# Second Hyena layer's intermediates in PSUM, and the seams of the one-stream layers

## The chip, the cores and the metric

One core of a Trainium2 chip runs the program once per execution. The metric is the device time of one execution in microseconds (us); the time before is the median of three runs. A profiled execution is a run by itself, with its own time.

## What is computed

A diffusion trunk of four layers over 256 latent tokens and 256 context tokens of width 1024, batch 1. Layers 0 and 3 mix tokens by a Hyena long convolution, layer 1 by gated linear attention, layer 2 by latent attention (MLA); an MLP follows each. Context tokens are last read in layer 2, so its MLP and all of layer 3 run on one stream, the 256 latent tokens. In short:

```python
for i in range(4):
    x = x + gate1[i] * mixer(modulate(rmsnorm(x), shift1[i], scale1[i]))
    x = x + gate2[i] * (relu(modulate(rmsnorm(x), shift2[i], scale2[i]) @ w1[i]) ** 2) @ w2[i]
out = rmsnorm(x) * final_g

def hyena(u):                      # layer 3: u is (256, 1024)
    z = short_conv(u @ w_in + b_in)            # three taps along the tokens, 3 x 1024 channels
    y, gates = z[:, :1024], (z[:, 1024:2048], z[:, 2048:])
    for n in range(2):
        y = gates[n] * (irfft(rfft(y, 512) * spectrum[n], 512)[:256] + y * skip[n])
    return y @ w_out + b_out
```

All inputs are fp32.

## The kernel before

**Layout.** x is kept transposed in SBUF, eight tiles `x0` to `x7` (`xT[k]`) of 128 channels x tokens. A product of fp32 accuracy is three matmuls: each operand is split into a rounded high part and the rest (`H` and `L`), and `mm3` (L368) adds high x high, high x rest and rest x high. `split` (L174) makes the parts: ScalarE casts, VectorE subtracts. Weights come as slabs of 128x1024 (`wload`): SP's DMA into `wraw`, a cast on ScalarE (L359, `wh`), a subtraction on GpSimd (L360, `wl`). PSUM's eight banks are dealt out by tags: two `mm`, three `cv`, one `ada`, two `st`. The compiler's scheduler sets each engine's order from the program's order and priorities; the order stands in the program, and every engine works through its own queue.

**One-stream norm.** `lone_norm` (before each of the three one-stream sub-layers) does not wait for 1/rms: it makes u = x * scale (parts `uH`, L553 on ScalarE, and `uL`, L554 on VectorE), squares x on ScalarE (L490), adds the squares on VectorE (`sacc`, L497), sums over channels by four small matmuls (L501), works out 1/rms on small tiles, and spreads it over the partitions by a matmul of `ones` with a diagonal matrix (L557), copied to `rs`. Each product of u and a weight has two columns more, for the shift; `modulated` then multiplies by `rs` (L567).

**Updates of x.** `residual` multiplies the mixer's output by the output weights, a bank `mm` for each 128 channels, and adds into x in SBUF (L600). In the one-stream MLP the second product is summed in four banks (`sum`, two halves of 256 each) over all 32 hidden slabs, and added into x in SBUF at the end (L677).

**Second Hyena layer.** `project` makes, for a unit of 256 channels, six products of 24 matmuls: VectorE scales into `zb` in SBUF (L567), ScalarE adds the bias (L880) and starts the convolution (L881), VectorE adds the two outer taps (L884, L886) into `z`. `order` transposes z (L912, L913 make `zf`), transforms it by matmuls with `dftf`, multiplies by the spectrum `S` on VectorE (L956, L957 into `pr`), subtracts and adds on GpSimd (L958, L959), splits into `VH`, `VL`, transforms back with `dftg` into a bank `st`, and gates (L983 to L985; L991 in the second order). Four units run in steps: step n projects unit n + 1, runs order 0 of unit n and order 1 of unit n - 1, and `residual` follows as units end.

## Time and profile before

| | |
|---|---|
| median of 3 runs | 2227.89 us (2223.2 to 2237.05) |
| the profiled execution | 2229.64 us, span 2227.9 us |
| TensorE (PE) busy | 2081.7 us, 93% |
| VectorE (DVE) busy | 1339.7 us, 60% |
| GpSimd (POOL) busy | 1122.9 us, 50% |
| ScalarE (ACT) busy | 907.9 us, 41% |
| from the end of MLA to the last MLP | 1640 to 2050 us of the span |

The shares are means over stages with different limits. The rows further down are of the trace of this one execution; times in them count from the start of its span. Matmuls are pipelined, and a matmul's row overlaps the next one's. A "wait" of an engine names the instruction that ended it.

### The profile page before, as it was taken

How to read it: one execution, taken by the hardware profiler on the slowest of the kernel's cores; microseconds unless marked ns; L12 is line 12 of the kernel's file. 1: busy time of each engine (PE TensorE's matmuls, PEld its weight loads, DVE VectorE, ACT ScalarE, POOL GpSimd, SP SyncE). 2: the span in 40 equal slices, each digit the busy share in tenths (PEclk: the TensorE clock that was granted, in tenths of full speed). 3: DMA queues.
4: the chain of work that ended last, by engine and by line, in shares of the span. 5: the costliest groups of instructions: out<-in, count | busy, mean ns of one | idle time of the engine just before them, and what ended most of it. 6: DMA issues, size and time to landing. Idle time of an engine off the chain costs nothing. (4 is left out here: it accounts for less than half of the span.)

```text
span 2227.9 us, 33311 instructions
## 1 busy us (share of the span) xinstructions
PE 2081.7 (93%) x12834; PEld 1773.8 (80%) x12834; DVE 1339.7 (60%) x2412; ACT 907.9 (41%) x1505; POOL 1122.9 (50%) x669
## 2 busy tenths in 40 slices
PE   6998999899999999998999999999989997887998
PEld 3765687677888888877778787788779997877998
DVE  7864887765333345555666976777662227995223
ACT  2642333343333335544442222236445445544544
POOL 5662454256544434322234434443347887674885
PEclk8998999999999999999999999999999997998999
DMA  9675735534333333222137797743236664343663
GB/s 300 198 222 189 228 99 180 193 94 123 97 109 108 96 77 96 60 66 66 48 103 228 216 306 242 252 142 91 73 104 180 181 189 138 117 121 90 189 186 114
DMA packets 322302, 329.12 MB, mean 148 GB/s; under 512 B 21277, under 2 KB 248674, under 8 KB 322144
## 3 DMA queue, kind: packets, MB, share of 16 engines
q1 hardware_dynamic: 321012, 326.05, 47.4%
q8 instruction: 101, 1.65, 0.3%
q10 hardware_dynamic: 587, 0.61, 0.1%
q14 instruction: 58, 0.47, 0.1%
q0 software_dynamic: 544, 0.34, 0.1%
HBM read 317.51 MB, written 9.44 MB: 147 GB/s over the span
## 5 line engine op out<-in xcount | busy, mean ns | idle before, releaser
L360 POOL TENSOR_TENSOR wl<-wraw,wh 128x1024 fp32r<-128x1024 f32 (+2 forms) x378 | 912.6, 2428 | 891.8 <-ACT wh L359 821.1
L359 ACT CAST wh<-wraw 128x1024 fp32r<-128x1024 f32 (+2 forms) x378 | 391.1, 1043 | 613.5 <-PE mm L370 245.7
L370 PE MATMUL mm<-uL,wh 128*128 128x512 f32 (+3 forms) x1288 | 454.3, 354 | 12.0 <-DVE uL L530 6.5
L369 PE MATMUL mm<-uH,wh 128*128 128x512 f32 (+3 forms) x1288 | 454.0, 356 | 11.4 <-DVE zb L567 5.1
L371 PE MATMUL mm<-uH,wl 128*128 128x512 f32 (+3 forms) x1288 | 450.5, 351 | 0.0
L369 PEld LDWEIGHTS mm<-uH,wh 128*128 128x128 f32 (+1 forms) x1288 | 249.4, 195 | 54.0 <-issue 12.8
L370 PEld LDWEIGHTS mm<-uL,wh 128*128 128x128 f32 (+1 forms) x1288 | 250.5, 195 | 46.4 <-DVE uL L530 10.7
L371 PEld LDWEIGHTS mm<-uH,wl 128*128 128x128 f32 (+1 forms) x1288 | 250.9, 195 | 32.3 <-issue 3.8
L369 PE MATMUL cv<-fH,wh 128*128 128x512 f32 (+1 forms) x576 | 210.0, 370 | 9.7 <-ACT fH L176 6.9
L370 PE MATMUL cv<-fL,wh 128*128 128x512 f32 (+1 forms) x576 | 210.7, 367 | 0.7 <-DVE fL L177 0.6
L371 PE MATMUL cv<-fH,wl 128*128 128x512 f32 (+1 forms) x576 | 208.9, 366 | 0.0
L600 DVE SCALAR_TENSOR_TENSOR x<-cv,mods,x 128x256 f32<-128x256 f32 x256 | 112.5, 479 | 83.9 <-PE cv L371 83.9
L370 PE MATMUL sum<-fL,wh 128*128 128x256 f32 x512 | 138.6, 278 | 0.0
L369 PE MATMUL sum<-fH,wh 128*128 128x256 f32 x512 | 137.1, 278 | 0.0
L371 PE MATMUL sum<-fH,wl 128*128 128x256 f32 x512 | 136.9, 278 | 0.0
L369 PEld LDWEIGHTS cv<-fH,wh 128*128 128x128 f32 x576 | 108.2, 189 | 32.0 <-ACT fH L176 8.5
L369 PE MATMUL mm<-oH,wh 128*128 128x256 f32 (+1 forms) x288 | 102.6, 358 | 23.7 <-DVE x L600 18.1
L648 DVE SCALAR_TENSOR_TENSOR mm<-mm,r 128x512 f32<-128x512 f32 x60 | 41.8, 696 | 136.7 <-ACT r L647 136.7
L370 PEld LDWEIGHTS cv<-fL,wh 128*128 128x128 f32 x576 | 108.6, 189 | 19.1 <-DVE fL L177 1.1
L371 PEld LDWEIGHTS cv<-fH,wl 128*128 128x128 f32 x576 | 108.6, 189 | 17.7 <-issue 0.2
L436 DVE SCALAR_TENSOR_TENSOR st<-lw,sT,st 128x512 f32<-128x512 f32 x144 | 101.7, 750 | 9.6 <-DMA lw<-in_ada_w_dram 9.6
L564 DVE COPY rbias<-st 128x1 f32<-128x1 f32 x32 | 5.1, 158 | 162.7 <-PE st L371 162.5
(479 smaller groups left out, 4561.9 us busy)
## 6 DMA issues: line engine op xcount, KB each, us to landing
wraw<-in_mlp_w_dram SPq DMA_DIRECT2D x256, 512.0 KB
adaw<-in_ada_w_dram SPq DMA_DIRECT2D x96, 512.0 KB
lw<-in_ada_w_dram SPq DMA_DIRECT2D x96, 512.0 KB
wraw<-in_hy_w_in_dram SPq DMA_DIRECT2D x48, 512.0 KB
wraw<-in_gla_w_in_dram SPq DMA_DIRECT2D x24, 512.0 KB
spec<-S SPq DMA_DIRECT2D x16, 512.0 KB
wraw<-in_hy_w_out_dram SPq DMA_DIRECT2D x16, 512.0 KB
S<-spec SPq DMA_DIRECT2D x32, 256.0 KB
```

The lines of the kernel that those rows point to most:

```text
L359: nc.scalar.copy(wh[r0:r1, :n], raw[r0:r1, :n])
L360: nc.gpsimd.tensor_tensor(wl[r0:r1, :n], raw[r0:r1, :n], rounded(wh[r0:r1, :n]), ALU.subtract)
L369: nc.tensor.matmul(ps, lh, rh, start=start, stop=False)
L370: nc.tensor.matmul(ps, lh, rl, start=False, stop=False)
L371: nc.tensor.matmul(ps, ll, rh, start=False, stop=stop)
L436: nc.vector.scalar_tensor_tensor(dst, wt[:, cols], sT[:, k, 0:1], run[b], ALU.mult, ALU.add)
L564: nc.vector.tensor_copy(bias, ps[:, SEQ : SEQ + 1])
L600: add = nc.vector.scalar_tensor_tensor(xT[dt][:, q], ps[:, q], mods[i][:, gi, dt, r : r + 1], xT[dt][:, q], ALU.mult, ALU.add)
L648: nc.vector.scalar_tensor_tensor(r, r, 0.0, pos, ALU.max, ALU.mult)
```

## The change

In layer 3's Hyena (`not two` in the code), `zb` is the product's own bank: the scaling, the bias and the taps read and write it there. The product with the spectrum writes its first half to an SBUF tile of half the size and its second half back into the bank of the transform; the subtraction and addition, on VectorE now, end in that bank, and it is split from there. The gated product and the last product likewise stay in their `st` banks. `off` is made in the two-stream layer alone.

At the end of MLA and of Hyena `residual_lone` sums the last 256 rows of the output product in the four `sum` banks. There, and at the end of layer 2's MLP, `add_gated` writes the new x into the bank in place of SBUF (`fresh`), and `lone_norm` reads it from there: `uH`, `uL`, the squares (summed in a bank `mm`), and a copy of each tile to SBUF on ScalarE. `statistics` and its `rstd` are functions now, and `behind_norm` calls them so that the statistics come behind the first product and the matmul of 1/rms behind the third. The steps on the products that need `rs` follow it. The last MLP still adds into SBUF.

```diff
+    def add_gated(i, gi, sums, dt, in_place):
+        for e in (dt - 1, dt):
+            sv = sums[dt // 2][:, e % 2]
+            nc.vector.scalar_tensor_tensor(sv if in_place else xT[e][:, :SEQ], sv, mods[i][:, gi, e, 0:1],
+                                           xT[e][:, :SEQ], ALU.mult, ALU.add)
+            if in_place:
+                fresh[e] = sv
+    def residual_lone(i, gi, wmat, r0, fH, fL):
+        sums = pairs()
...
+                for k in range(2):
+                    mm3(sums[dt // 2][:, dt % 2], wh[:, k, cols], wl[:, k, cols], fH[k][:, :SEQ], fL[k][:, :SEQ],
+                        k == 0 and dt % 2 == 0, k == 1 and dt % 2 == 1)
+                if dt % 2 == 1:
+                    add_gated(i, gi, sums, dt, True)
     def lone_norm(i, which, mp):
...
-            nc.scalar.activation(uH[k][:, :SEQ], xT[k][:, :SEQ], AF.Copy, scale=sc)
-            nc.vector.scalar_tensor_tensor(uL[k][:, :SEQ], xT[k][:, :SEQ], sc, rounded(uH[k][:, :SEQ]),
+            nc.scalar.activation(uH[k][:, :SEQ], fresh[k], AF.Copy, scale=sc)
+            nc.vector.scalar_tensor_tensor(uL[k][:, :SEQ], fresh[k], sc, rounded(uH[k][:, :SEQ]),
                                            ALU.mult, ALU.subtract)
-        rb = bank("st")
-        nc.tensor.matmul(rb[:, :SEQ], ones, token_diag(token_rstd(0)), start=True, stop=True)
+        run = bank("mm")[:, :SEQ]
+        acc = np_.tile([P, SEQ], F32, tag="sacc", name=nm("sacc"), bufs=1)
+        for k in range(KD):
+            sq = np_.tile([P, SEQ], F32, tag="sq", name=nm("sq")) if k else None
+            nc.scalar.activation(sq if k else run, fresh[k], AF.Square)
+            if 0 < k < KD - 1:
+                nc.vector.tensor_tensor(acc if k == KD - 2 else run, run, sq, ALU.add)
+        for k in range(KD):
+            nc.scalar.copy(xT[k][:, :SEQ], fresh.pop(k))
...
+    def behind_norm(products, statistics, rest):
+        made = [products[0]()]
+        rstd = statistics()
+        made += [p() for p in products[1:]]
+        rstd()
+        return [rest(m) for m in made]
...
+                def convolved(made):
...
+                    zb = (mp.tile([P, 512], F32, tag="zb", name=nm("zb")) if two else ps)[:, :nt]
...
                         else:
+                            pr = mq.tile([P, 2, 256], F32, tag="pr1", name=nm("pr"))
+                            re, im = (pv[:, e : e + 1].broadcast_to([P, 2, 2, P]) for e in range(2))
+                            nc.vector.tensor_tensor(pr.rearrange("p r (a c) -> p r a c", a=2), re, s1, ALU.mult)
+                            nc.vector.tensor_tensor(pv, im, s2, ALU.mult)
+                            V2 = ps.rearrange("p (r c) -> p r c", r=2)
+                            nc.vector.tensor_tensor(V2[:, 0], pr[:, 0], V2[:, 0], ALU.subtract)
+                            nc.vector.tensor_tensor(V2[:, 1], pr[:, 1], V2[:, 1], ALU.add)
+                            split(V2, VH, VL)
...
+                            nc.vector.tensor_tensor(pr, even, gate, ALU.mult)
+                            nc.vector.tensor_tensor(eo, odd, gate[:, 1::-1], ALU.mult)
+                            nc.vector.tensor_tensor(eo, pr, eo, ALU.add)
+                            split(eo, *mids[cts[0]])
                     else:
+                        y = z[2] if two else acc
...
-                        split(z[2], h, l)
+                        split(y, h, l)
...
+                                if n == units - 1:
+                                    residual_lone(i, 2, g["hy_w_out"][j], n * 2 * P, *f)
...
-                    residual(i, 2, g["mla_wo"][j], pair * 2 * VD, oH, oL, SEQ)
+                    residual_lone(i, 2, g["mla_wo"][j], pair * 2 * VD, oH, oL)
```

**The order on PE at seam 1** (end of MLA into layer 2's MLP). Before, PE has this around the matmul of 1/rms; `mm_14944` and `mm_15026` are the first two products of the MLP, `st_14985` the third:

```order
L371 MATMUL mm_14944<-uH_14853,wl_14939 128x258
L369 MATMUL mm_15026<-uH_14851,wh_15020 128x258
L370 MATMUL mm_15026<-uL_14859,wh_15020 128x258
L371 MATMUL mm_15026<-uH_14851,wl_15021 128x258
L369 MATMUL mm_15026<-uH_14852,wh_15020 128x258
L370 MATMUL mm_15026<-uL_14860,wh_15020 128x258
L371 MATMUL mm_15026<-uH_14852,wl_15021 128x258
L369 MATMUL mm_15026<-uH_14853,wh_15020 128x258
L370 MATMUL mm_15026<-uL_14861,wh_15020 128x258
L371 MATMUL mm_15026<-uH_14853,wl_15021 128x258
L557 MATMUL st_14894<-diag_14931,ones 128x256
L369 MATMUL st_14985<-uH_14846,wh_14979 128x258
```

In the changed kernel PE has the end of the first product (`mm_14928`), the four statistics matmuls, and the start of the second product (`st_14976`):

```order
L370 MATMUL mm_14928<-uL_14857,wh_14923 128x258
L371 MATMUL mm_14928<-uH_14849,wl_14924 128x258
L603 MATMUL st_14953<-ones,sacc_14891 128x2
L603 MATMUL st_14953<-ones,sq_14911 128x2
L603 MATMUL st_14953<-ones,sacc_14891 128x2
L603 MATMUL st_14953<-ones,sq_14911 128x2
L369 MATMUL st_14976<-uH_14842,wh_14971 128x258
```

and, 48 rows behind the statistics, the end of the third product (`mm_15007`), 1/rms and the start of the fourth:

```order
L369 MATMUL mm_15007<-uH_14849,wh_15002 128x258
L370 MATMUL mm_15007<-uL_14857,wh_15002 128x258
L371 MATMUL mm_15007<-uH_14849,wl_15003 128x258
L610 MATMUL st_14953<-diag_14967,ones 128x256
L369 MATMUL st_15070<-uH_14842,wh_15065 128x258
```

The statistics stood some 37 matmuls behind the first product's start, with 11 left to do before 1/rms; now they stand 24 behind it, with 48 in between. Seam 3 has the same pattern.

**The order on ScalarE at seam 2** (layer 2's MLP into Hyena). Before, the last dozen rows up to the last square, which reads the last x tile; `wh` are casts of weights:

```order
L553 ACTIVATE uH_17231<-x_185,adam_11771 128x256
L553 ACTIVATE uH_17232<-x_186,adam_11771 128x256
L490 ACTIVATE sq_17285<-x_183 128x256
L1032 ACTIVATE x_181<-x_181,gb_18275 128x256
L490 ACTIVATE sq_17288<-x_184 128x256
L1032 ACTIVATE x_182<-x_182,gb_18278 128x256
L176 CAST dftf_17319<-traw_17321 128x512
L176 CAST dftg_17325<-traw_17327 128x512
L490 ACTIVATE sq_17291<-x_185 128x256
L359 CAST wh_17495<-wraw_17494 128x1024
L359 CAST wh_17534<-wraw_17533 128x1024
L490 ACTIVATE sq_17294<-x_186 128x256
```

Now, in the same place (L584 makes `uH`, L592 squares, L596 copies x to SBUF, L1145 adds the output bias):

```order
L176 CAST dftg_17315<-traw_17317 128x512
L584 ACTIVATE uH_17236<-sum_15149,adam_11771 128x256
L592 ACTIVATE sq_17289<-sum_15148 128x256
L592 ACTIVATE sq_17292<-sum_15148 128x256
L596 COPY x_183<-sum_15148 128x256
L596 COPY x_184<-sum_15148 128x256
L1145 ACTIVATE x_181<-x_181,gb_18266 128x256
L1145 ACTIVATE x_182<-x_182,gb_18269 128x256
L176 CAST dftg_17315<-traw_17321 128x512
L592 ACTIVATE sq_17295<-sum_15149 128x256
L359 CAST wh_17499<-wraw_17498 128x1024
L592 ACTIVATE sq_17298<-sum_15149 128x256
```

The copies have come in between; one weight cast fewer stands ahead of the last square, and that square is one row behind a cast whose buffer the first product frees.

**The order on VectorE in Hyena**, at the third product of unit 2 (`mm_17975` before, `mm_17969` now). Before, the product's bank is read for the last time by L567; `zb_17976` is in SBUF:

```order
L566 TENSOR_TENSOR zbias_18001<-mm_17975,params 128x1
L567 TENSOR_TENSOR zb_17976<-mm_17975,rs_17314 128x256
L956 TENSOR_TENSOR pr_18221<-cv_18214,S_18129 128x512
L957 TENSOR_TENSOR pr_18221<-cv_18214,S_18129 128x512
L886 SCALAR_TENSOR_TENSOR z_17889<-zb_17936,params,z_17889 128x255
L177 TENSOR_TENSOR VL_18198<-pr_18192,VH_18197 128x512
L912 TENSOR_TENSOR zf_18459<-z_17889 128x256
L913 TENSOR_TENSOR zf_18459<-z_17889 128x256
L884 SCALAR_TENSOR_TENSOR z_17968<-zb_17976,params,z_17968 128x255
```

Now L971 is its last reader:

```order
L620 TENSOR_TENSOR zbias_17995<-mm_17969,params 128x1
L971 SCALAR_TENSOR_TENSOR z_17917<-mm_17931,params,z_17917 128x255
L621 TENSOR_TENSOR mm_17969<-mm_17969,rs_17308 128x256
L1093 TENSOR_TENSOR pr_18254<-st_18233,z_17686 128x512
L1003 TENSOR_TENSOR zf_18446<-z_17917 128x256
L1004 TENSOR_TENSOR zf_18446<-z_17917 128x256
L1094 TENSOR_TENSOR st_18233<-st_18233,z_17686 128x512
L969 SCALAR_TENSOR_TENSOR z_17994<-mm_17969,params,z_17994 128x255
L1095 TENSOR_TENSOR st_18233<-pr_18254,st_18233 128x512
L971 SCALAR_TENSOR_TENSOR z_17994<-mm_17969,params,z_17994 128x255
```

A bank `mm` that was free one row after L566 is now free nine rows after L620.

## Rows read from the trace of the kernel before

In the first group busy times stand in the order PE, PE's weight loads, DVE, ACT, POOL, each with its number of instructions.

**Rows 1.** Stretches: start:end, length, busy by engine, granted clock, DMA share, GB/s

```profile
1640.00:1672.00 32.00, 23.26 (x157) 22.06 (x157) 21.82 (x42) 15.17 (x32) 14.20 (x7) 0.84 0.42 132
1700.00:1800.00 100.00, 100.00 (x850) 100.00 (x850) 24.04 (x64) 48.79 (x68) 82.18 (x36) 1.00 0.62 183
1838.00:1868.00 30.00, 20.73 (x112) 19.83 (x111) 20.54 (x31) 16.49 (x33) 18.78 (x12) 0.66 0.45 133
1868.00:2014.00 146.00, 120.06 (x919) 115.50 (x917) 134.63 (x213) 70.13 (x109) 100.41 (x76) 0.95 0.42 123
2014.00:2050.00 36.00, 27.62 (x181) 26.39 (x182) 22.95 (x46) 16.34 (x34) 13.77 (x6) 0.81 0.22 65
```

**Rows 2.** PE's waits from 1868 to 2014: total us, times, longest

```profile
PE st L370 <- DVE VL L177: 7.6, 4, 3.2
PE mm L369 <- DVE zb L567: 5.8, 4, 2.4
```

**Rows 3.** VectorE by line and shape, 1868 to 2014: count, busy us, mean ns, idle before

```profile
L177 DVE TENSOR_TENSOR VL<-pr,VH 128x512 fp32r<-128x512 f32 x16 | 21.4, 1341 | 1.4 <-ACT VH L176 1.3
L886 DVE SCALAR_TENSOR_TENSOR z<-zb,params,z 128x255 f32<-128x255 f32 x24 | 20.6, 866 | 0.2
L884 DVE SCALAR_TENSOR_TENSOR z<-zb,params,z 128x255 f32<-128x255 f32 x24 | 16.5, 687 | 4.1 <-ACT z L881 4.0
...
L985 DVE TENSOR_TENSOR pr<-pr 128x512 f32<-128x512 f32 x4 | 7.0, 1738 | 0.0
...
L177 DVE TENSOR_TENSOR yL<-pr,yH 128x512 fp32r<-128x512 f32 x4 | 2.7, 678 | 0.0
...
L177 DVE TENSOR_TENSOR yL<-cv,yH 128x512 fp32r<-128x512 f32 x3 | 2.1, 684 | 0.1
```

**Rows 4.** VectorE in order of time, 1886 to 1899: start, us, what

```profile
1891.91 0.41 DVE L567 TENSOR_TENSOR zb<-mm,rs 128x256 f32<-128x256 f32 x1
1892.24 2.26 DVE L886 SCALAR_TENSOR_TENSOR z<-zb,params,z 128x255 f32<-128x255 f32 x1
...
1897.21 0.48 DVE L886 SCALAR_TENSOR_TENSOR z<-zb,params,z 128x255 f32<-128x255 f32 x1
```

**Rows 5.** GpSimd in order of time, the same stretch

```profile
1891.40 2.81 POOL L360 TENSOR_TENSOR wl<-wraw,wh 128x1024 fp32r<-128x1024 f32 x1
1898.30 2.40 POOL L360 TENSOR_TENSOR wl<-wraw,wh 128x1024 fp32r<-128x1024 f32 x1 [4.08 <-ACT wh L359]
```

**Rows 6.** PE's waits at seam 1, 1640 to 1672

```profile
PE st L557 <- DVE diag L510: 5.4, 1, 5.4
PE mm L369 <- DVE x L600: 3.3, 4, 1.9
```

**Rows 7.** PE's waits at seam 2, 1838 to 1868

```profile
PE mm L370 <- DVE uL L554: 5.3, 2, 2.8
PE st L501 <- DVE sacc L497: 4.0, 1, 4.0
```

**Rows 8.** PE's waits at seam 3, 2014 to 2050

```profile
PE st L557 <- DVE diag L510: 5.9, 1, 5.9
PE mm L369 <- DVE x L600: 2.0, 2, 1.8
```

**Rows 9.** ScalarE by line and shape, 1836 to 1869: count, busy us, mean ns, idle before

```profile
L359 ACT CAST wh<-wraw 128x1024 fp32r<-128x1024 f32 x7 | 7.2, 1039 | 5.3 <-PE ada L370 3.3 <-PE mm L370 2.0
...
L559 ACT COPY rs<-st 128x256 f32<-128x256 f32 x1 | 0.4, 374 | 0.0
```

**Rows 10.** ScalarE, then PE, in order of time at seam 2

```profile
1836.19 0.51 ACT L553 ACTIVATE uH<-x,adam 128x256 fp32r<-128x256 f32 x1 [3.91 <-DVE x L677]
1836.61 0.40 ACT L490 ACTIVATE sacc<-x 128x256 f32<-128x256 f32 x1
...
1859.48 0.59 PE L501 MATMUL st<-ones,sacc 128*128 128x2 f32 x2 [3.95 <-DVE sacc L497]
...
1866.94 1.06 PE L557 MATMUL st<-diag,ones 128*128 128x256 f32 x2
```

More of the change, by code (lines that the diff above doesn't have):

```diff
@@ L539, in norm_mod, with pairs @@
         return uH, uL
+    fresh = {}
+    def pairs():
+        return [pp.tile([P, 2, SEQ], F32, tag=t, name=nm("sum"), bufs=banks[t]) for t in ("cv", "cv", "cv", "ada")]
+    def add_gated(i, gi, sums, dt, in_place):
[7 more added lines that the diff above has]
+        sums = pairs()
+        for c in range(2):
+            wh, wl = wload(wmat[r0 : r0 + 2 * P, c * 512 : (c + 1) * 512].rearrange("(k p) c -> p k c", p=P), [P, 2, 512])
+            for d in range(4):
+                dt = 4 * c + d
+                cols = slice(d * P, (d + 1) * P)
+                for k in range(2):
[3 more added lines that the diff above has]
+                    add_gated(i, gi, sums, dt, True)
     def lone_norm(i, which, mp):
@@ L623, in mlp @@
             if single:
-                u, modulated = lone_norm(i, 1, mp)
+                u, statistics, modulated = lone_norm(i, 1, mp)
             if later is not None:
@@ L652, in hidden @@
                 return h, l
+            def hidden(c):
+                return squared(first_product(c))
             pump(8)
@@ L661, in accumulate @@
                 if grp == 0:
-                    sums.extend(pp.tile([P, 2, SEQ], F32, tag=t, name=nm("sum"), bufs=banks[t])
-                                for t in ("cv", "cv", "cv", "ada"))
+                    sums.extend(pairs())
                 for c in range(2):
@@ new lines, in project, with product @@
+                early = unit == 0 and not two
+                tiles = {}
+                def product(part, a):
+                    w = wcols(g["hy_w_in"][j], (part * KD + cts[a]) * P)
+                    if early and part * nct + a < 4:
+                        ps = bank(("mm", "st")[a])
+                    else:
+                        ps = bank("cv" if unit == 0 and part == 2 and not build else "mm")
+                    if two:
+                        gemm_T(ps[:, :nt], w, u, nt, halves=unit == 0)
+                    else:
+                        gemm_T(ps[:, : SEQ + 2], w, u, SEQ + 2)
+                    return part, a, ps
@@ new lines, in convolved @@
+                def convolved(made):
+                    part, a, ps = made
+                    if part not in tiles:
+                        tiles[part] = mp.tile([P, 512], F32, tag=f"z{part}", name=nm("z"), bufs=3 if part or two else 2)
+                        z.append(tiles[part])
+                    ch = part * KD + cts[a]
+                    zb = (mp.tile([P, 512], F32, tag="zb", name=nm("zb")) if two else ps)[:, :nt]
+                    dst = tiles[part][:, a * nt : (a + 1) * nt]
+                    cw = [pc("hy_conv_w", q * 3 * KD + ch, j) for q in range(3)]
+                    b_in = pc("hy_b_in", ch, j)
+                    if two:
+                        nc.scalar.activation(zb, ps[:, :nt], AF.Identity, bias=b_in)
+                        nc.scalar.activation(dst, ps[:, :nt], AF.Identity, scale=cw[1], bias=off[:, ch : ch + 1])
+                    else:
+                        b = mp.tile([P, 1], F32, tag="zbias", name=nm("zbias"))
+                        modulated(ps, zb, b, b_in)
+                        nc.scalar.activation(zb, zb, AF.Identity, bias=b)
+                        nc.scalar.activation(dst, zb, AF.Identity, scale=cw[1], bias=pc("hy_conv_b", ch, j))
+                    dv = dst.rearrange("p (s t) -> p s t", t=SEQ)
+                    zv = zb.rearrange("p (s t) -> p s t", t=SEQ)
+                    nc.vector.scalar_tensor_tensor(dv[:, :, 1:], zv[:, :, : SEQ - 1], cw[0], dv[:, :, 1:],
+                                                   ALU.mult, ALU.add)
+                    nc.vector.scalar_tensor_tensor(dv[:, :, : SEQ - 1], zv[:, :, 1:], cw[2], dv[:, :, : SEQ - 1],
+                                                   ALU.mult, ALU.add)
@@ L890, in hyena @@
+                todo = [(part, a) for part in parts_ for a in range(nct)]
+                if early:
+                    behind_norm([lambda t=t: product(*t) for t in todo[:3]], statistics, convolved)
+                    todo = todo[3:]
+                for t in todo:
+                    convolved(product(*t))
             live = {}
```

124 lines of the change are left out of this document (60 added, 64 removed).

## Prediction

> **What bounds the kernel now.** I read the table of stretches first. A reference stretch in a layer's MLP, 1700 to 1800 [rows 1], has TensorE without a pause: 850 matmuls in 100 us, 0.118 us each, at a granted clock of 1.00 (the 2.4 GHz level). At that pace the matmuls of the other stretches would need 157 x 0.118 = 18.5 us of 32 (end of MLA into its MLP, "seam 1"), 112 x 0.118 = 13.2 of 30 (that MLP into the second Hyena layer, "seam 2"), 919 x 0.118 = 108 of 146 (the second Hyena layer), 181 x 0.118 = 21.3 of 36 (Hyena into the last MLP, "seam 3") [rows 1]. So 13.5 + 16.8 + 38 + 14.7 = 83 us lie above TensorE's own work. No gain can be larger. Part of it is the clock, which lies between the two levels (1.2 and 2.4 GHz) where TensorE waits: 0.66, 0.81 and 0.84 in the seams, 0.95 in Hyena.
>
> In the Hyena stretch VectorE is busy 134.6 us of 146 [rows 1], and PE's longest waits there end with VectorE: on `VL` and on `zb` [rows 2]. VectorE is the bound. But its work is dearer than it need be. By groups of lines [rows 3], a subtraction over 512 elements takes 0.678 us as `yL<-pr` and 1.341 us as `VL<-pr`; L886 takes 0.866 us in the mean. In order of time [rows 4, 5]: GpSimd splits a weight from 1891.40 to 1894.21; L567, whose one input is in PSUM, runs in 0.41 us at 1891.91 in spite of it; L886, both inputs in SBUF, starts at 1892.24 and lasts 2.26 us, to 0.3 us past GpSimd's end. At 1897.21, with GpSimd out of the way, the same L886 takes 0.48 us. Two tensor inputs in SBUF are what is held up.
>
> At the seams [rows 6, 7, 8] PE waits for 1/rms (`diag`, 5.4 and 5.9 us) and for the updated x (3.3 and 2.0) at seams 1 and 3, and for `uL` (5.3) and the sum of squares (4.0) at seam 2.
>
> **The change, part by part.**
>
> Hyena. The intermediates `zb`, `V`, the gated product and the last product go to PSUM, so L886, L884, `VL` and L985 read one SBUF tensor at most. Held time that goes, by [rows 3] against 0.48 and 0.678 us: `VL` 16 x (1.341 - 0.678) = 10.6; L886 24 x (0.866 - 0.48) = 9.3; L884 24 x (0.687 - 0.48) = 5.0; L985 4 x (1.738 - 0.678) = 4.2. Sum 29.1 us. Added: the 32 subtractions and additions of 128x256 that GpSimd did come to VectorE. Nearest row: L567, same shape, one input in PSUM, 0.41 us; its neighbour starts 0.33 us after it [rows 4]. 32 x 0.33 to 0.41 = 10.6 to 13.1, say 12. Net 17 us of VectorE's 134.6. The real and imaginary products keep their number and shape, and so do `zf` and its holding up. For ops on PSUM in place I take the SBUF price: `yL<-cv` reads PSUM in 0.684 us, `yL<-pr` SBUF in 0.678 [rows 3].
>
> The Trainium skill speaks against that price. Its page "VectorE: DVE Perf Modes", section "The TRN2 errata", gives a VectorE instruction from PSUM 62 cycles at 0.96 GHz more than one from SBUF, by estimate 0.065 us. About 118 instructions move (48 of the short convolution, 28 subtractions and sums, 42 at the seams): some 8 us, and the sum below would be 25 instead of 33. The rows just named show 6 ns; I go by them.
>
> Is the 17 us on the path? VectorE idles only 11.4 us of the stretch. After the change it needs some 118 us there, PE 108. They are close, and neither hides the other wholly: I take 17, with 0 below (the first rival) and 29 above (the added work falling into pauses, and fewer low-clock stretches).
>
> GpSimd loses 32 instructions. It was not late: worth nothing itself. ScalarE's steps move to PSUM at one for one; its casts of `VH` no longer wait for GpSimd, which is latency that the last unit, where nothing overlaps, gets back; I count it in the upper end. `off` (two tiny VectorE instructions in seam 2) is dropped where it isn't read.
>
> Seams. On PE the matmul of 1/rms goes behind the second and third product, but the four statistics matmuls now stand right behind the first (order rows), where PE waits for the last square. What is late next is therefore the square. At seams 1 and 3, from the last matmul of the new `sum` on: two updates 0.9, then on that bank `uH`, `uL`, `uH`, `uL` one after another at about 0.5 each (a row of the same shape has 0.51 [rows 10], L886 0.48), 2.9 us; then ScalarE has six squares and four copies (x back to SBUF) up to the last square. A square takes 0.40 [rows 10], a copy 0.37 [rows 9], and a start follows the one before 0.1 us sooner than its end (1836.19 and 0.51, then 1836.61 [rows 10]): 6 x 0.40 + 4 x 0.37, less 10 x 0.1, is 2.9; the last addition 0.4. In all 6.2 us, of which the first product covers 24 x 0.118 = 2.8: a wait of 3.4. Behind it, two products (5.6 us) cover the chain to `diag`, which has nothing left to hide but a few small instructions. Seam 1: 5.4 + 1.9 (the longest of the waits for x) - 3.4 = 4 us. Seam 3: 5.9 + 2.0 - 3.4 = 4.5 us.
>
> Seam 2. Here ScalarE's queue sets the square: from the first `uH` to the last square it has, by order, 8 `uH`, 4 weight casts, 8 squares, 6 copies, 4 bias additions and 3 table casts: 8 x 0.51 + 4 x 1.04 + 8 x 0.40 + 6 x 0.37 + 4 x 0.51 (the bias additions have the shape of `uH`) + 3 x 0.6 (512 elements, between the copy of 256 and the cast of 1024) = 17.5, less 0.1 for each of 33 = 14.2 us [rows 9, 10]. From 1836.19 that is 1850.4; before, the statistics began at 1859.48 [rows 10]. PE then owes 48 + 6 matmuls up to 1/rms: 6.4 us at full clock, 12.7 at half, so 1856.8 to 1863. Before it was 1866.94 [rows 10]. Gain 4 to 10; I take 7. `uL` is no longer held (5.3 us); that is inside this.
>
> Sum: 17 + 4 + 7 + 4.5 = 32.5 us. The profiled execution took 2229.6 us (span 2227.9 and 1.7 around it), so 2197; the median of the runs, 2227.9, lies 1.7 lower: **2195 us**.
>
> **Rivals.**
> (a) The two `mm` banks bound Hyena. A product's bank was given back after L567; now it is held until L971, which reads `zb` last. In the order rows L620 of `mm_17969` comes first and its L971 is ninth behind it; at the prices above these take some 4 us. With hold H a pair of banks passes a product each (2.8 + H)/2 us. Now it is 146/24 = 6.1. With H = 9.4 (4 in VectorE's queue, the rest behind weight casts of 1.04 us on ScalarE and the `zf` that are held up still) the gain in Hyena is gone: 33 - 17, 2212. For: the wait for `zb` already is PE's second [rows 2]. Against: products have 10 to 30 other matmuls between them. Chance 0.13.
> (b) Slower: the same mechanism, with H above 9.4 + 2 x 15.5/24 = 10.7 us, where it eats the seams' gain too. At H = 13, 24 x 7.9 = 190 us instead of 146: 2228 + 44 - 15 = 2257. Against: nothing in the order makes so long a hold. Chance 0.05.
> (c) The seams give nothing: the wait for 1/rms only turns into one for the squares, because ScalarE has eight copies more and takes turns with VectorE on each bank. If ScalarE's queue behind the last `uH` holds two weight casts too (2.1 us) and the turns cost double (2.1), each seam loses about 4 more: 15.5 - 12 = 3.5 left, 2207. The Trainium skill's page "PSUM — Partial Sum Buffer", section on bank collisions, says that no two engines may touch one bank at a time, reads included; by that rule these turns are forced. Chance 0.08.
> (d) The change doesn't do what it says: instructions that read PSUM are still held up, since they write `z` or `VL` in SBUF. Then 29 stays and 12 comes on top: 2228 + 12 - 15 = 2225. Against: L567 wrote SBUF and wasn't held [rows 4]. Chance 0.02.
>
> **How the numbers follow.** Forecast 0.72. Its bounds: Hyena 5 to 29, seams 8 to 24: 13 to 53 us, 2175 to 2215. This takes in (a) and (c); (b) and (d) and the tails are left out: 2174 to 2214 for 8 in 10. About 1%, 22 us, is what a measurement here can tell from no change. Faster by more: the forecast with a little over 22 us, 0.74 with the good edge of (c). Within 1%: (a), the rest of (c), (d), 0.20. Slower: (b) and accidents, 0.06.
>
> **What would show it.** VectorE in Hyena: the convolution steps near 0.48 us and `VL` near 0.68, also beside a weight split; a stretch near 129 us. PE's waits at the seams: on the sum of squares, 3 to 4 us, none on `diag`. In seam 2 statistics near 1850 on the old time line. Wrong would be: PE waiting on L971 for more than 10 us in sum (a), statistics waits over 6 us (c), or `VL` still above 1 us (d).

## The result: 2198.9 us, and where the time came from

The changed kernel takes 2198.93 us (median; 2194.1 to 2204.9) against 2229.71 us before in the runs beside it: ratio 0.9862, interval 0.9822 to 0.9903, so 31 us or 1.4% faster.

To compare stages I cut every profiled run at the same matmuls: the start of the last attention product of MLA, of the last matmul of layer 2's MLP sum, of 1/rms in the second Hyena layer, of its last transform back, and of the 101st sum matmul of the last MLP. Seam 1 lies in the first stretch (with layer 2's MLP), seam 2 is the second, then comes Hyena, then seam 3 with the start of the last MLP. The table of stretches of the kernel before, with these cuts (columns as in [rows 1]):

```profile
1635.60:1840.60 205.00, 196.26 (x1621) 194.92 (x1621) 71.90 (x168) 100.75 (x157) 156.76 (x82) 0.98 0.57 172
1840.60:1866.90 26.30, 17.03 (x85) 16.31 (x84) 18.27 (x30) 12.86 (x27) 16.21 (x11) 0.63 0.51 150
1866.90:2012.10 145.20, 120.84 (x921) 116.31 (x920) 133.76 (x211) 70.54 (x108) 100.41 (x76) 0.95 0.41 121
2012.10:2073.00 60.90, 50.94 (x378) 49.51 (x378) 30.00 (x65) 28.33 (x51) 32.85 (x14) 0.89 0.37 112
```

and of the changed kernel:

```profile
1639.00:1837.00 198.00, 193.65 (x1612) 192.09 (x1611) 65.80 (x172) 101.38 (x163) 157.34 (x82) 0.99 0.59 177
1837.00:1858.30 21.30, 14.41 (x89) 13.00 (x88) 10.03 (x25) 15.56 (x38) 12.45 (x11) 0.76 0.55 161
1858.30:1983.90 125.60, 113.44 (x893) 108.69 (x892) 108.84 (x239) 65.57 (x107) 64.77 (x43) 0.99 0.48 139
1983.90:2044.10 60.20, 53.03 (x402) 51.10 (x401) 29.65 (x69) 30.57 (x61) 37.81 (x16) 0.94 0.41 124
```

A reader should look at three things. First, the cuts do not hold the same matmuls: in the changed kernel 9 fewer lie behind the first cut, 4 more in seam 2, 28 fewer in Hyena and 24 more behind it. The last two stretches are therefore read together, and differences are mended by 0.118 us per matmul: seam 1 loses 7.0 - 1.1 = 5.9 us, seam 2 5.0 + 0.5 = 5.5, Hyena with seam 3 (206.1 to 185.8) 20.3 - 0.5 = 19.8. Together 31.2 us, all of the gain. Secondly, the program ahead of the first cut, which the change hardly touches, took 1635.6 and 1639.0 us: profiled runs differ there by some microseconds (1630.8 to 1639.0 over all kernels below), so the spans show less than the stretches do. Thirdly, GpSimd's busy time in Hyena falls from 100 to 65 us and VectorE's from 134 to 109, and the clock rises from 0.95 to 0.99.

VectorE by line and shape in the Hyena stretch of the changed kernel (answering [rows 3]; L969 and L971 are the outer taps, L621 the scaling, L1061 the subtraction that came from GpSimd, whose addition L1062 took as long):

```profile
L1003 DVE TENSOR_TENSOR zf<-z 128x256 f32<-128x256 f32 x8 | 10.9, 1367 | 0.1
L969 DVE SCALAR_TENSOR_TENSOR z<-mm,params,z 128x255 f32<-128x255 f32 x20 | 9.5, 476 | 3.0 <-ACT z L966 2.7
L971 DVE SCALAR_TENSOR_TENSOR z<-mm,params,z 128x255 f32<-128x255 f32 x20 | 9.5, 475 | 0.1
...
L177 DVE TENSOR_TENSOR VL<-cv,VH 128x512 fp32r<-128x512 f32 x13 | 8.8, 681 | 0.5 <-ACT VH L176 0.5
L621 DVE TENSOR_TENSOR mm<-mm,rs 128x256 f32<-128x256 f32 x20 | 8.5, 425 | 3.7 <-ACT rs L611 3.5
L1061 DVE TENSOR_TENSOR cv<-pr,cv 128x256 f32<-128x256 f32 x13 | 5.2, 418 | 0.0
```

The taps fell from 0.866 and 0.687 to 0.48 us, `VL` from 1.341 to 0.681. Only `zf`, left with two SBUF inputs, is still dear.

PE's waits at seam 1, at seam 2 and at seam 3 (answering [rows 6], [rows 7] and [rows 8]):

```profile
PE st L603 <- DVE rbias L618: 1.4, 1, 1.4
PE mm L370 <- DVE uL L585: 1.1, 3, 0.5
PE mm L369 <- ACT uH L584: 1.0, 1, 1.0
```

```profile
PE mm L369 <- ACT uH L584: 3.5, 2, 1.9
PE st L603 <- DVE sacc L594: 2.8, 1, 2.8
PE mm L370 <- DVE uL L585: 0.6, 2, 0.4
```

```profile
PE st L610 <- DVE diag L510: 3.7, 1, 3.7
...
PE st L603 <- DVE sacc L594: 0.9, 1, 0.9
```

The wait for `diag` (1/rms) is gone at seam 1; at seam 3, 3.7 of 5.9 us are still there. The prediction had not foreseen that, and e7 to e9 are about it. (L618 in the first row is the copy of one column that stands right behind the last addition of squares, so this is the wait for the squares.)

### The profile page after: what moved, and what is told of

Same layout as the page of the kernel before. It is cut to its first block, busy times and chain, and to the rows that moved or that the text cites. A ratio compares the mean times of both kernels' runs of the same rounds, so it can differ in the third digit from the quotient of the medians.

```text
span 2199.0 us, 33332 instructions
## 1 busy us (share of the span) xinstructions
PE 2076.9 (94%) x12834; PEld 1767.8 (80%) x12834; DVE 1300.7 (59%) x2442; ACT 907.8 (41%) x1529; POOL 1088.2 (49%) x637
## 5 line engine op out<-in xcount | busy, mean ns | idle before, releaser
L369 PE MATMUL mm<-uH,wh 128*128 128x512 f32 (+3 forms) x1272 | 449.4, 356 | 15.0 <-ACT uH L584 5.4
L370 PE MATMUL mm<-uL,wh 128*128 128x512 f32 (+3 forms) x1272 | 449.3, 354 | 8.5 <-DVE uL L530 5.8
L371 PE MATMUL mm<-uH,wl 128*128 128x512 f32 (+3 forms) x1272 | 444.7, 351 | 0.0
L369 PEld LDWEIGHTS mm<-uH,wh 128*128 128x128 f32 (+1 forms) x1272 | 245.0, 194 | 58.2 <-issue 8.7
L371 PEld LDWEIGHTS mm<-uH,wl 128*128 128x128 f32 (+1 forms) x1272 | 245.9, 193 | 32.5 <-issue 3.8
L369 PE MATMUL mm<-oH,wh 128*128 128x256 f32 (+1 forms) x256 | 92.0, 361 | 18.9 <-DVE x L663 14.2
L618 DVE COPY rbias<-st 128x1 f32<-128x1 f32 x32 | 5.1, 159 | 163.1 <-PE st L371 162.8
```

The costliest lines, as they stand in the source:

```text
L369: nc.tensor.matmul(ps, lh, rh, start=start, stop=False)
L370: nc.tensor.matmul(ps, lh, rl, start=False, stop=False)
L371: nc.tensor.matmul(ps, ll, rh, start=False, stop=stop)
L618: nc.vector.tensor_copy(bias, ps[:, SEQ : SEQ + 1])
```

## The experiments

The theory (H): VectorE's instructions with two tensor inputs in SBUF stand still while GpSimd runs a weight split, and the change gains in Hyena because it takes one of the two inputs to PSUM; at the seams the later matmul of 1/rms and the update in PSUM give the rest. Medians beside the kernel before on the same chip, ratios with their interval, and stretches of the profiled run, cut as above:

| kernel | median, before | ratio | seam 1 + MLP | seam 2 | Hyena + seam 3 |
|---|---|---|---|---|---|
| before | | | 205.0 | 26.3 | 206.1 |
| changed | 2198.9, 2229.7 | 0.9862 (0.9822 to 0.9903) | 198.0 | 21.3 | 185.8 |
| e1 Hyena part alone | 2208.6, 2228.1 | 0.9916 (0.9901 to 0.9931) | 205.3 | 26.1 | 188.5 |
| e2 seams alone | 2211.9, 2228.1 | 0.9938 (0.9921 to 0.9956) | 199.1 | 21.4 | 198.6 |
| e3 zb in SBUF | 2218.1, 2228.1 | 0.9957 (0.9942 to 0.9972) | 198.6 | 21.1 | 205.8 |
| e4 V in SBUF | 2199.9, 2228.1 | 0.9878 (0.9860 to 0.9897) | 198.0 | 23.1 | 187.9 |
| e5 V on GpSimd | 2198.2, 2227.9 | 0.9865 (0.9847 to 0.9884) | 199.2 | 21.2 | 189.7 |
| e6 1/rms one product later | 2198.7, 2227.9 | 0.9864 (0.9847 to 0.9881) | 196.8 | 22.3 | 185.6 |
| e7 other chain to diag | 2189.2, 2227.9 | 0.9828 (0.9813 to 0.9843) | 198.0 | 22.0 | 182.0 |
| e8 before, other chain | 2221.7, 2226.5 | 0.9975 (0.9963 to 0.9988) | 201.8 | 26.3 | 204.3 |
| e9 other chain and zf | 2180.2, 2226.5 | 0.9794 (0.9773 to 0.9814) | 198.6 | 21.5 | 170.4 |
| e10 x in SBUF | 2204.0, 2227.9 | 0.9901 (0.9880 to 0.9921) | 201.5 | 21.8 | 188.4 |
| e11 before, no rests | 2197.5, 2226.5 | 0.9866 (0.9845 to 0.9887) | 205.3 | 21.8 | 178.5 |
| e12 changed, no rests | 2202.2, 2228.5 | 0.9885 (0.9864 to 0.9905) | 198.5 | 24.7 | 187.0 |

### The two parts apart: e1 and e2

e1 is the kernel before with the Hyena part alone, e2 the changed kernel without it:

```diff
 e1, against the kernel before
-                        zb = mp.tile([P, 512], F32, tag="zb", name=nm("zb"))
+                        zb = mp.tile([P, 512], F32, tag="zb", name=nm("zb")) if two else ps
...
 e2, against the changed kernel
-                    zb = (mp.tile([P, 512], F32, tag="zb", name=nm("zb")) if two else ps)[:, :nt]
+                    zb = mp.tile([P, 512], F32, tag="zb", name=nm("zb"))[:, :nt]
...
```

> The kernel before with the Hyena part of the change alone (zb, V, eo and y in PSUM); the seams stay as they were. Theory H (VectorE's steps with two SBUF inputs are held up by GpSimd, and their cost ends the Hyena stretch): the taps fall to 0.48 us and VL to 0.68 us in the mean, VectorE's busy time in the Hyena stretch falls by 15 to 20 us, the stretch from the matmul of 1/rms to the last transform back falls from 145.5 us to 126 to 130, the whole to 2210 to 2214 us; the waits for diag at seams 1 and 3 stay at 5 to 6 us. Rival S (the seams brought the gain and Hyena is no faster): 2225 us or more.

> The changed kernel with Hyena's intermediates in SBUF as before and the subtraction and addition on GpSimd again; only the seams are new. Theory H: the Hyena stretch is as long as before (143 to 148 us), taps 0.69 to 0.87 us, VL 1.3 us; the seams give 12 to 16 us, the whole 2212 to 2217 us. Rival S (the seams are the whole gain): 2199 us. Rival c (the seams give nothing): 2225 us or more.

e1 took 19.6 us off the median and 17.6 off its stretch; e2 16.3 off the median, 5.9, 4.9 and 7.5 off the three stretches. The median of e1 lies 1.4 us below its range, and VectorE's busy time fell by 24.4 us there, more than the 15 to 20 expected. The theories that give nothing to one of the parts fall, S and c. The two gains in the stretches, 17.6 and 18.3, are 36 us together and the whole change has 32. The missing 4 us are at seam 3: in e2 the code that makes `diag` there is the same as in the changed kernel, but PE did not wait for it, since GpSimd's split happened to fall elsewhere (the next one starts at 2021.62, when `diag` is made):

```profile
2020.53 0.16 DVE L476 SCALAR_TENSOR_TENSOR rst<-rsy 128x2 f32<-128x2 f32 x1 [0.51 <-ACT rsy L475]
```

### What in Hyena brought it: e3, e4 and e5

Each takes one part of the Hyena change back: `zb` to SBUF (e3); the result of the subtraction and addition to SBUF, still on VectorE (e4); that step wholly as before, with GpSimd (e5).

```diff
 e3
-                    zb = (mp.tile([P, 512], F32, tag="zb", name=nm("zb")) if two else ps)[:, :nt]
+                    zb = mp.tile([P, 512], F32, tag="zb", name=nm("zb"))[:, :nt]
 e4
-                            V2 = ps.rearrange("p (r c) -> p r c", r=2)
+                            W = ps.rearrange("p (r c) -> p r c", r=2)
+                            V2 = mq.tile([P, 2, 256], F32, tag="V2", name=nm("V2"))
...
 e5
+                        nc.gpsimd.tensor_tensor(pr[:, 0, 0], pr[:, 0, 0], pr[:, 0, 1], ALU.subtract)
+                        nc.gpsimd.tensor_tensor(pr[:, 1, 0], pr[:, 1, 0], pr[:, 1, 1], ALU.add)
+                        split(pr[:, :, 0], VH, VL)
```

> The changed kernel with zb alone in SBUF again: a product's bank is free after the scaling, and the two taps read two SBUF tensors. Theory H: the taps go back to a mean of 0.69 to 0.87 us, VectorE's busy time in Hyena rises by about 14 us and the stretch by 9 to 14: 2208 to 2213 us. Rival a (the hold of the two mm banks costs more than the taps gain): 2199 us or less.

> The changed kernel with the results of the subtraction and addition (V) in an SBUF tile, still made on VectorE: VL reads two SBUF tensors again, and nothing else changes. Theory H: VL goes from 0.68 to about 1.3 us, 16 times, VectorE's busy time rises by about 10 us, and the Hyena stretch by 5 to 10: 2204 to 2209 us. Rival P (what helped was that GpSimd's subtraction and addition left the chain): 2199 us, as the changed kernel.

> The changed kernel with the step behind the spectrum wholly as before: both products in an SBUF tile, subtraction and addition on GpSimd, VL from SBUF. zb, eo and y stay in PSUM. Theory H, by VectorE's busy time alone: it loses 32 x 0.42 = 13 us and gains 16 x 0.66 = 11 us of held VL, so the whole is the same within 3 us, 2196 to 2202 us. Rival L (latency: GpSimd's two instructions take 0.9 us each and queue behind weight splits, and PE waits for VL): PE's waits on VL come back to 7 us or more, the stretch from 1/rms to the last transform grows by 5 to 10 us, the whole is 2204 to 2209 us.

VectorE's groups in the Hyena stretch: two of e3, one of e4, one of e5.

```profile
L969 DVE SCALAR_TENSOR_TENSOR z<-zb,params,z 128x255 f32<-128x255 f32 x24 | 25.9, 1079 | 4.2 <-ACT z L966 4.2
L971 DVE SCALAR_TENSOR_TENSOR z<-zb,params,z 128x255 f32<-128x255 f32 x24 | 22.8, 951 | 0.2
```

```profile
L177 DVE TENSOR_TENSOR VL<-V,VH 128x512 fp32r<-128x512 f32 x16 | 16.1, 1014 | 1.0 <-ACT VH L176 1.0
```

```profile
L177 DVE TENSOR_TENSOR VL<-pr,VH 128x512 fp32r<-128x512 f32 x16 | 21.1, 1319 | 0.0
```

In e3 the taps cost 48.7 us in place of 48 x 0.476 = 22.8, and the stretch is 20 us longer: nearly all of Hyena's gain hangs on `zb`. What PE waits for there is the scaling, which stands behind the taps in VectorE's queue:

```profile
PE mm L369 <- DVE zb L621: 12.5, 8, 3.1
```

It is more than theory H had priced (9 to 14 us), because the held share isn't a constant: GpSimd is busy 70 us there, before 100, and yet the taps are held longer than in [rows 3]. What counts is what a tap meets, and when. Tap by tap, before: of 48, 21 start while GpSimd is at work, 12 of these in a weight split, 1.3 us behind its start in the mean, 9 in one of GpSimd's shorter instructions; 16 last over 0.6 us. In e3 18 start so, 17 of them in a split, 0.7 us behind its start in the mean, and these 17 last over 0.6 us. In the changed kernel 22 start so, and none lasts over 0.6 us. Wherever it began, each of the 16 and of the 17 ends 0.28 or 0.29 us behind GpSimd's instruction. At worst a tap and a split start together, so that it waits for nearly all of it; VectorE and GpSimd of e3 in order of time:

```profile
1892.36 2.62 DVE L969 SCALAR_TENSOR_TENSOR z<-zb,params,z 128x255 f32<-128x255 f32 x1
1895.01 0.48 DVE L971 SCALAR_TENSOR_TENSOR z<-zb,params,z 128x255 f32<-128x255 f32 x1
...
1898.12 2.63 DVE L971 SCALAR_TENSOR_TENSOR z<-zb,params,z 128x255 f32<-128x255 f32 x1
```

```profile
1892.25 2.45 POOL L360 TENSOR_TENSOR wl<-wraw,wh 128x1024 fp32r<-128x1024 f32 x1 [1.10 <-ACT wh L359]
1898.10 2.38 POOL L360 TENSOR_TENSOR wl<-wraw,wh 128x1024 fp32r<-128x1024 f32 x1 [3.39 <-ACT wh L359]
```

For rival a of the prediction e3 gives the net: its `mm` banks are free right after the scaling, and it is slower all the same.

e4 missed its number. `VL` is held again (1.01 us, 5.3 us in sum, half of what was expected), but the time is that of the changed kernel within the intervals. That is rival P's number; but e5, which gives the step back to GpSimd, has it too, so P falls as well. e5 came out as theory H's sum by busy time had it, 2198.2 us; its profiled stretch is 3.9 us longer than the changed kernel's, less than the 5 to 10 of rival L, and PE waits for `VL` there 1.0 us in all. So the step behind the spectrum, which in the prediction stood for 10.6 us of gain and 12 of cost, is worth between nothing and 4 us, and the gated product and the last product can hold no more than what is left.

### GpSimd taken away: e11 and e12

The direct test leaves all data where they are and removes GpSimd's splits. In the second Hyena layer ScalarE writes a scaled copy of the weight where its rest should be (so the rest is another number):

```diff
+        if lite[0]:
+            nc.scalar.activation(wl[r0:r1, :n], raw[r0:r1, :n], AF.Copy, scale=2.0 ** -12)
+        else:
+            nc.gpsimd.tensor_tensor(wl[r0:r1, :n], raw[r0:r1, :n], rounded(wh[r0:r1, :n]), ALU.subtract)
```

> The kernel before, but in the second Hyena layer GpSimd makes no rests of weights: ScalarE writes a scaled copy of the weight in their place, so the rest is another number, and all else is computed as before. Data stay where they were, in SBUF. Theory H (GpSimd's work holds up VectorE's steps with two SBUF inputs): with GpSimd's 70 us of splits gone from the stretch, the taps fall from 0.69 and 0.87 to 0.5 to 0.6 us and VL from 1.34 to 0.7 to 1.0 us (the subtractions and additions of V stay on GpSimd), and VectorE's busy time falls by 15 us or more. Rival W (two SBUF inputs are slower by themselves, or transfers slow them): the means stay within 0.1 us of before.

> The changed kernel with the same edit as in e11: in the second Hyena layer ScalarE writes a scaled copy of each weight in the place of its rest, and GpSimd makes none. In the kernel before that edit alone gave as much as the whole change. Theory H (what the change's Hyena part gains is freedom from GpSimd's hold-ups, so it can't be had twice): of VectorE's steps only zf is left to be freed, 1.37 to 0.42 us, 8 times; the stretch from 1/rms to the last transform falls from 125.6 us by 4 to 9 us, the whole to 2189 to 2196 us. Rival D (GpSimd's splits and the place of the intermediates are two separate costs): the two gains add, 2165 to 2175 us.

The groups of e11 in its Hyena stretch (L890 and L892 are the taps on SBUF's `zb`):

```profile
L890 DVE SCALAR_TENSOR_TENSOR z<-zb,params,z 128x255 f32<-128x255 f32 x24 | 13.0, 541 | 3.6 <-ACT z L887 3.5
L892 DVE SCALAR_TENSOR_TENSOR z<-zb,params,z 128x255 f32<-128x255 f32 x24 | 13.0, 545 | 0.4
L177 DVE TENSOR_TENSOR VL<-pr,VH 128x512 fp32r<-128x512 f32 x16 | 12.0, 754 | 0.0
```

With two SBUF inputs as before, the taps take 0.54 us and `VL` 0.75. VectorE's busy time falls from 133.8 to 95.4 us, and the kernel before, with its old seams, reaches 2197.5 us. Its seam 2 is shorter too: `uL` and the sums of squares take 0.48 and 0.42 us there in place of 0.73 and 1.14, and of PE's 9.3 us of waits on them [rows 7] 0.2 are left. Rival W falls: neither SBUF itself nor transfers made these steps dear, GpSimd's work did. This is what the Trainium skill has on its page "SBUF — State Buffer", section "Who interferes with whom": a VectorE instruction with two SBUF inputs contends with a GpSimd instruction that reads SBUF, and the one that comes second is blocked. The trace agrees (2.62 us against 0.48). How much of the 29 us in the whole comes by way of VectorE isn't told apart, since the rests come from another engine too.

In e12 the gains do not add: 2202.2 us, as the changed kernel, so rival D falls. But theory H's number was missed too. `zf` is free (0.41 us, expected 0.42) and VectorE is down to 102 us, yet the stretch is 133.3 us, not 117 to 122. ScalarE has 26 copies of weights more there (busy 88 us against 66). But that is not the whole reason, for e11 has the same load. The Hyena stretches of e11 and of e12 (columns as in [rows 1]):

```profile
1860.50:1978.50 118.00, 109.72 (x873) 107.48 (x874) 95.38 (x207) 89.74 (x131) 27.92 (x48) 0.97 0.48 141
1857.10:1990.40 133.30, 118.76 (x893) 114.11 (x892) 102.19 (x239) 88.47 (x133) 2.72 (x16) 0.94 0.44 131
```

The 20 matmuls more are 2.4 of the 15.3 us. PE's longest waits in Hyena of e12:

```profile
PE mm L374 <- DVE z L977: 6.1, 5, 3.9
PE cv L374 <- ACT yH L176: 3.7, 2, 3.1
```

L977 is the second tap, the last reader of a product's bank. In e11 a bank is free after the scaling, for which PE waits 3.1 us. So the longer hold that rival a named has a price: in the changed kernel PE waits 3.8 us on that tap, in e5 7.3. It was outweighed there by what the taps gained. Where no split holds them up, the intermediates in PSUM brought nothing here; how much of the remaining 13 us is the hold, and how much the other differences of the two kernels, isn't shown.

A number for the changed kernel without GpSimd's splits and without more work on ScalarE wasn't taken.

### The seams: e6, e10

e6 asks for 1/rms right behind the statistics; e10 writes the new x to SBUF, where `lone_norm` reads it.

```diff
 e6
-        made += [p() for p in products[1:]]
         rstd()
+        made += [p() for p in products[1:]]
 e10
-                    add_gated(i, gi, sums, dt, True)
+                    add_gated(i, gi, sums, dt, False)
...
-            nc.scalar.copy(xT[k][:, :SEQ], fresh.pop(k))
+            fresh.pop(k)
```

> The changed kernel with the matmul of 1/rms right behind the statistics, ahead of the second and third product; the updates in PSUM stay. Theory O (it is the order that hides the chain to diag): PE waits for diag at all three seams, 3.5 us or more at seam 1, 1.9 at seam 2, about 7 at seam 3, of which 3.65 were there already; with the lower clock behind them 8 to 12 us in all: 2207 to 2211 us. Rival I (the updates in PSUM bring the seams' gain): 2202 us or less.

> The changed kernel with the new x written to SBUF, as before, and lone_norm reading it there (no copies back on ScalarE, uL with two SBUF inputs); sums, order of the statistics and 1/rms stay. Theory I (the update in PSUM matters): uL is held up, 1 us or more in the mean against 0.48, and each seam loses 1 to 3 us: 2202 to 2208 us. Rival B (turns of ScalarE and VectorE on one bank and the copies cost as much as they bring): 2195 to 2200 us.

e6 didn't do what it was meant to do. The compiler's scheduler moved the second product ahead of 1/rms by itself, so that 28, 28 and 27 matmuls lie between the last statistics and 1/rms at the three seams; in the changed kernel it is 48, 37 and 27. What it shows is that one product is enough at seams 1 and 2: PE doesn't wait for `diag` there, and the time is the same. The case with nothing in between remains untried; the nearest to it is the kernel before, with 11 matmuls and a wait of 5.4 us at seam 1.

e10 is slower than the changed kernel by some 5 us in the median (2204.0), in the stretches 3.5 at seam 1, 0.5 at seam 2, 2.6 in the last. `uL` at seam 1, first of the changed kernel, then of e10:

```profile
L585 DVE SCALAR_TENSOR_TENSOR uL<-sum,adam,uH 128x256 fp32r<-128x256 f32 x8 | 3.5, 476 | 0.4 <-ACT uH L584 0.4
```

```profile
L584 DVE SCALAR_TENSOR_TENSOR uL<-x,adam,uH 128x256 fp32r<-128x256 f32 x8 | 6.9, 904 | 0.2 <-ACT uH L583 0.2
```

`uL` with x in SBUF is held to 0.904 us, and PE waits for it 4.2 us there, against 1.1. Theory I holds for seam 1 and in the sum, and rival B falls with it, though the intervals of the two ratios overlap and the case rests mainly on the rows. At seam 2 PE waits 5.5 us for `uL` in e10 and the stretch is only 0.5 us longer, so freeing `uL` is hardly what shortened that seam.

### What was late at seam 3: e7, e8, and a faster kernel, e9

VectorE and then GpSimd at seam 3 of the changed kernel, in order of time:

```profile
2006.87 2.34 DVE L476 SCALAR_TENSOR_TENSOR rst<-rsy 128x2 f32<-128x2 f32 x1 [0.95 <-ACT rsy L475]
2009.24 0.16 DVE L477 TENSOR_TENSOR rst<-rst,rsv 128x2 f32<-128x2 f32 x1
2009.44 0.16 DVE L478 SCALAR_TENSOR_TENSOR rsy<-rst,rsy 128x2 f32<-128x2 f32 x1
2009.63 2.57 DVE L510 TENSOR_SCALAR diag<-ident,rsy 128x128 f32<-128x128 f32 x2
```

```profile
2006.81 2.38 POOL L360 TENSOR_TENSOR wl<-wraw,wh 128x1024 fp32r<-128x1024 f32 x1 [3.89 <-ACT wh L359]
2009.69 2.43 POOL L360 TENSOR_TENSOR wl<-wraw,wh 128x1024 fp32r<-128x1024 f32 x1 [0.49 <-ACT wh L359]
```

A step over 128x2 elements takes 2.34 us, and ends with GpSimd's split. The same had made up most of the waits for 1/rms of [rows 6] and [rows 8]; before, at seam 1:

```profile
1658.42 1.21 DVE L476 SCALAR_TENSOR_TENSOR rst<-rsy 128x2 f32<-128x2 f32 x1 [2.04 <-ACT rsy L475]
1659.67 2.26 DVE L477 TENSOR_TENSOR rst<-rst,rsv 128x2 f32<-128x2 f32 x1
```

e7 (on the changed kernel) and e8 (on the kernel before) write that chain so that no step of VectorE has two SBUF tensors:

```diff
+        nc.scalar.activation(yy, y, AF.Square)
+        nc.vector.scalar_tensor_tensor(t, yy, -0.5, v, ALU.mult, ALU.mult)
+        nc.vector.scalar_tensor_tensor(r, t, 1.5, y, ALU.add, ALU.mult)
+        diag = np_.tile([P, 2, P], F32, tag="sq", name=nm("diag"))
+        for j in range(2):
+            nc.scalar.activation(diag[:, j], ident, AF.Copy, scale=r[:, j : j + 1])
```

Here `yy` and `t` are columns of the statistics' PSUM bank. e9 has this and another `zf`: ScalarE copies the backward half of z into the bank that the transposes write later, and VectorE adds and subtracts from there.

```diff
+                        back = ps[:, : 2 * P].rearrange("p (a c) -> p a c", c=P)
+                        nc.scalar.copy(back, yv[:, :, SEQ - 1 : P - 1 : -1])
+                    nc.vector.tensor_tensor(zf[:, 0], yv[:, :, :P], back, ALU.add)
```

> The changed kernel with the small chain from the sum of squares to diag in another form at the three seams: the square of y on ScalarE into PSUM, two VectorE steps in place of three, each with one SBUF tensor at most, and diag made by two ScalarE steps. Theory G (the tiny steps of 128x2 take up to 2.3 us because GpSimd's weight split holds up every VectorE step with two SBUF inputs): the steps take 0.16 to 0.2 us each; at seam 3 the wait for diag falls from 3.65 to under 1 us; the whole 2194 to 2198 us. Rival Q (the chain is late by the weight casts ahead of it on ScalarE): the wait stays at 2 us or more.

> The kernel before with the small chain from the sum of squares to diag in the other form (square of y on ScalarE into PSUM, two VectorE steps with one SBUF tensor at most, diag on ScalarE), and nothing else. Theory G (GpSimd's weight splits hold up the tiny VectorE steps, and that is most of the wait for 1/rms): the waits for diag at seams 1 and 3 fall from 5.4 and 5.9 us to about 2 to 3.5 us, the whole by 5 to 8 us: 2220 to 2224 us. Rival Q (the weight casts on ScalarE are what is late): the waits stay above 4.5 us, 2226 us or more.

> The changed kernel with the other form of the small chain at the seams and with zf from one PSUM and one SBUF input: ScalarE copies the backward half of z into the bank that the transposes write later. Theory H: zf falls from 1.37 us to 0.42 us in the mean for the first of its two steps, VectorE's busy time in Hyena falls by 7 us more, and the stretch by 3 to 6 us: 2190 to 2195 us. Rival E (PE, with 114 us of matmuls in the stretch, and the added 0.4 us of ScalarE ahead of each transpose decide by now): the stretch is as long as in the changed kernel, 2195 to 2200 us.

The chain in e7 at seam 3, VectorE and then ScalarE:

```profile
2003.76 0.17 DVE L578 SCALAR_TENSOR_TENSOR st<-st,rsv 128x2 f32<-128x2 f32 x1 [1.15 <-ACT st L577]
2003.96 0.16 DVE L579 SCALAR_TENSOR_TENSOR rst<-st,rsy 128x2 f32<-128x2 f32 x1
```

```profile
2004.16 0.69 ACT L582 ACTIVATE diag<-ident,rst 128x128 f32<-128x128 f32 x2 [0.43 <-DVE rst L579]
```

GpSimd runs a split from 2003.49 to 2005.89 beside them, and the steps take 0.17 us. The wait for `diag` is gone, and the last stretch (from the last transform on) falls from 60.2 to 56.4 us: the 3.7 that were missing. The median, 2189.2 us, fell by more than this accounts for, and below the 2194 to 2198 expected (9.8 us against the changed kernel's, with intervals that overlap). I count 4 us as shown; where the rest comes from is open. In e8 the waits fell from 5.4 and 5.9 to

```profile
PE st L574 <- ACT diag L554: 2.5, 1, 2.5
```

at seam 1 and 2.9 at seam 3, and the median by 4.9 us. So about 3 us of each of the two waits were GpSimd's doing (at seam 1 the rows above have 1.21 and 2.26 us for two steps of 0.16); what is left is two weight casts on ScalarE that stand in the chain. Theory G holds, Q has the smaller half.

In e9 `zf` takes 0.41 us:

```profile
L1022 DVE TENSOR_TENSOR zf<-z,cv 128x256 f32<-128x256 f32 x5 | 2.1, 413 | 0.5 <-ACT cv L1021 0.5
```

and the Hyena stretch is 116.7 us against 125.6, PE's 886 matmuls at 0.118 being 104.5. (e7, with as many matmuls, has 125.6 too, so this is `zf` alone.) The median is 2180.2 us: below both kernels, and its interval lies clear of the changed kernel's. It gained more than expected (theory H had 3 to 6 us in Hyena, it was 8.9); rival E falls.

## Why the prediction was right, and where its steps were off

**The sum.** Forecast 2195, measured 2198.9. Hyena: forecast 17, e1's stretch shows 17.6. Seam 1: 4, measured 5.9. Seam 2: 7, measured 5.5. Seam 3: 4.5, measured 2.2 in the changed kernel (19.8 less e1's 17.6) and about 7 in e2, where no split fell on the chain. That the sum came so close is in part luck: the seams' misses of +1.9, -1.5 and -2.3 us cancel in part, and in e1 VectorE's busy time fell by 24.4 us and not by 17, of which the time shows 17.6. The mechanism of the Hyena term is shown from both sides, by e3 (the data put back) and by e11 (GpSimd taken away).

**Hyena's parts.** The prices were right: taps at 0.48, `VL` at 0.68, the last sum of the gated product at 0.69; by rows 29 us of held time went, and 32 x 0.418 = 13.4 us were added (forecast 12). The split among them on the path was not: I took VectorE's busy time as if every microsecond counted alike. By e3 to e5, `zb` carries some 20 us, the step behind the spectrum at most 4. The taps stand between one product and the next, where PE waits on the bank and ScalarE on the scaling; `VL` was covered, as far as e5 shows: held again, it makes PE wait 1.0 us. I had also left `zf` as it was; it fell from 20.2 to 14.2 us while GpSimd's busy time fell from 100 to 65.

**PSUM's price.** I took the SBUF price for operands in PSUM, against the page "VectorE: DVE Perf Modes" of the Trainium skill (section "The TRN2 errata"), by which each would cost, by estimate, 0.065 us more. The rows bear the SBUF price out: the taps take 0.475 us from PSUM, and from SBUF 0.48 where GpSimd was out of the way [rows 4], `VL` 0.681 from PSUM against 0.678 for `yL<-pr` [rows 3]; the scaling in place took 0.425 against 0.41 [rows 4]. Nothing here shows 0.065.

**Seams 1 and 2.** The wait moved from `diag` to the squares as forecast, and was smaller (1.4 at seam 1 for 3.4), with 2.1 us more on `uH` and `uL`, which the sum had not listed: 3.5 in all, the forecast's total by another division. At seam 2 the statistics began 11.9 us behind the MLP's sum, before 18.9; the forecast had 9.8. It went by ScalarE's queue alone and overlooked a hold-up there too. In the chain that ended last, before, the last addition of squares at seam 2 is

```profile
1856.94 2.50 DVE sacc L497
```

beside a split; with the running sum in a bank it takes 0.42 us.

**Seam 3, the step that failed.** "Behind it, two products (5.6 us) cover the chain to `diag`, which has nothing left to hide but a few small instructions" is wrong in both halves. Only 27 matmuls stand behind the last statistics there (I carried the 48 of seam 1 over, and wrote that the pattern was the same), and the chain took over 5 us from its first VectorE step on, by the rows above. The hold-up is what left the 3.7 us: without it, in e7, the same 27 matmuls cover the chain. I had the means to see it: the hold-up that I had read at a tap (2.26 us for 0.48) applies to the tiny steps too, and a timeline of VectorE inside the waits of [rows 6] would have shown them. I read those waits as latency and looked for cover, when about 3 of 5.4 us could be had by another form of the chain (e8).

**The rivals.** (a) fell as a bound: PE's waits that end with L971 or `zbias` come to 6.7 us in Hyena, and e3, with the banks free early, is slower. The hold itself has a price (e12, beside e11). (b) and (d) fell too, by the groups of VectorE above. (c) fell: the seams give 13.6 us in the changed kernel and 16.3 by e2's median. The Trainium skill's page "PSUM — Partial Sum Buffer", section on bank collisions, forbids two engines one bank at a time. The steps are no dearer for such turns (`uL` takes 0.476 us in the bank that ScalarE reads too); whether PE's 2.1 us of waits on `uH` and `uL` come from them isn't shown.

## What to carry to other kernels

Where an engine seems to be the bound, compare the mean time of its instructions with their shortest: a mean of 0.87 us against 0.48 says that something else holds them, and a timeline names it. Then look for the same hold-up wherever a chain is waited for, in steps of a few elements above all, since they cost as much as large ones when held. Moving one of two inputs to PSUM frees a step; but price it by whether somebody waits behind that step, not by busy time, and set against it that the bank is held longer.
